# First mixer of a two-layer trunk: single-block loads behind modulation units, all units on VectorE, and norms whose roots are taken on 128x2

## The chip, the cores and the metric

The kernel runs on one core of one Trainium2 chip. The metric is the device time of one execution in microseconds (us), median of several runs; less is better. The engines are TensorE (PE, with its weight loads as PEld), VectorE (DVE), ScalarE (ACT), GpSimd (POOL) and SyncE (SP), which here only issues DMAs. Every engine takes its instructions in the order in which the program has them.

## The reference, cut to what matters

```python
for l in range(2):
    mod = (silu(c) @ ada_w[l] + ada_b[l])            # 6 vectors of 1024: sh1, sc1, g1, sh2, sc2, g2
    h = rmsnorm(x, norm_mix[l]) * (1 + sc1) + sh1
    if l % 2 == 0:                                   # first mixer
        proj = h @ ev_w_in                           # 1024 -> 1536: z (gated) and pool input
        ya = spatial_gating(gelu(proj[:, :512]), gelu(proj[:, 512:1024]))
        yb = multiscale_pool(proj[:, 1024:])
        y = concat(ya, yb) @ ev_w_out
    else:
        y = diff_attention(h, ...)
    x = x + g1 * y
    h = rmsnorm(x, norm_ffn[l]) * (1 + sc2) + sh2
    x = x + g2 * peer(h, ...)                        # queries h @ w_q, 16384 experts
out = rmsnorm(x, final_norm)
```

There are 256 tokens of width 1024, all in f32. `rmsnorm` divides each token by the root of its mean square over the 1024 features.

## The kernel before

**Layout.** `xt` holds x with the features on the partitions: 8 chunks `c` of 128 features by 256 tokens. Weights come from HBM as a stream of blocks of 128x1024 (512 KB). Blocks 0 to 11 are `ev_w_in`, 12 to 19 `ev_w_out`, 20 to 35 the `w_q` of the first expert stage. Blocks below 20 (`WHOLE`) are used as f32; every later one is split first into `hi` (a cast on ScalarE, L195) and `lo` (a subtraction on VectorE, L202), and each product then takes three matmuls. There are seven block buffers in this stage: a load of block k goes out when block k-7 has been used.

**Modulation units.** The first layer's `ada_w` comes in 24 units of 1 MB; the first mixer uses 0 to 19. In VectorE's form (`ada_next`, `ada_use`, L315) a unit costs two passes over 128x1024 with a running sum and two or three tiny instructions (`mod_done`). Units 0 to 7 give shift and scale for chunk c of the first norm, 8 to 11 the gates, 12 to 19 shift and scale of the second norm. Units 14 and 16 (`PE_UNITS`) are taken another way: `ada_rows` multiplies them on TensorE as rows, `ada_copy` moves the rows out, `ada_turn` turns them into columns. There are five unit buffers.

**Order of the loads.** The list `loads` sets what SyncE issues: `a5` is unit 5, `w6` the pair of blocks 12 and 13, `s0` the four small tensors. `issue` walks it as far as buffers are free in program order. SyncE has one queue: a load that waits for its buffer holds all those behind it.

**The stage around the change.** SyncE loads, `Norm` squares x on ScalarE and sums over the features with matmuls by a matrix of ones, so that `ss` is 128x256 with the same row on every partition; `rstd` takes root (L378) and reciprocal (L379) there. For each chunk c VectorE takes unit c and `hmod` (L585), ScalarE adds the shift (`hf`, L586), TensorE does the 12 products of `project`. Then come the gating (`vnorm`, `gating`), the pool sums (`pool_adds`, `pool_sums`) and `out_proj`. In `run_blocks` the first `lead` blocks go together, chunk by chunk: four of `ev_w_out` here, six of `w_q` (blocks 20 to 25) in the expert stage. The other four blocks of `out_proj` follow one by one, and for each finished output chunk `done` updates `xt` (L421) and squares it. `renorm` takes the second norm and `modulate`: per chunk `hmod` (L401) on VectorE, `hh[0]` on ScalarE (L403), `hh[1]` on VectorE (L394). `between` splits the last blocks ahead of the modulation, so that all six leading blocks are split when `modulate` begins.

Norms stand at five places: twice in each layer, and at the end of the kernel, where five of the eight output chunks are scaled on VectorE (L1253) and three on ScalarE and GpSimd (L1251).

Of the kernel before, what the change touches and what calls it, by code (L numbers as in the profile page):

```python
# [20 lines left out]
P = 128  # L21
# [20 lines left out]
NRAW = 4  # L42
PE_UNITS = (14, 16)
WHOLE = 20
# [3 lines left out]
def trunk(ctx, tc, xT, crow, vecs, consts_in, pos, lamv, bs, cnt, ws, wpool, ada, ev_in, ev_out,  # L48
# [293 lines left out]
    class Norm:  # L342
# [17 lines left out]

        def square(self, c):
            if self.last:
                self.add()
            q = self.buf(c)
            nc.scalar.activation(q, xt[:, c, :], AF.Square)
            self.last = (c, q)

        def sums(self):
            while self.sq:
                self.n += 1  # L370
                self.ss = self.ss if self.n > 1 else aux()
                mm(self.ss[:, :S], ones, self.sq.pop(0), self.n == 1, self.n == min(NCH, 1 + NCH - self.first))

        def rstd(self, work):
            self.add()
            self.sums()
            r = work.tile([P, S], F32, name="rstd", bufs=1)
            nc.scalar.activation(r, self.ss[:, :S], AF.Sqrt, bias=epst, scale=1.0 / D)  # L378
            nc.vector.reciprocal(r, r)  # L379
            return r  # L380

# [28 lines left out]

    def renorm(norm, l, m, work, before=None, between=None):
        r = norm.rstd(work)
        if between:
            between()
        modulate(r, l, m, work, before)

# [15 lines left out]
    def mixer0(work):  # L432
# [6 lines left out]
        cnt_t = work.tile([P, 4, 16], F32, name="cnt")  # L439
        adaq, consumed, rows = {}, set(), {}  # L440

        def small():
# [4 lines left out]

        loads = ("a0 w0 a1 w1 a8 a2 w2 a3 a9 a4 w3 a5 w4 a10 a6 w5 a7 a11 s0 w6 w7 a12 a13 w8 w9 a14 a15 a16 "
                 "w10 a17 w11 a18 a19 w12").split()
        slots = [int(v[1:]) for v in loads if v[0] == "a"]  # L450

        def issue():

            while loads:
                kind, un = loads[0][0], int(loads[0][1:])
                if kind == "s":
                    small()
                elif kind == "a":
                    n = slots.index(un)
                    if n >= 5 and slots[n - 5] not in consumed:  # L460
                        return
                    r = (work if n % 5 < 3 else adag).tile([P, 2, D], F32, name=f"adaw{n % 5}")
                    dma(r, ada[0, un].rearrange("p (a b) -> p a b", a=2))
                    adaq[un] = r
                else:
                    fetch(2 * un + 1)
                    if head["unit"] < 2 * un + 2:
                        return
                loads.pop(0)
            head.update(issue=None, ahead=3)  # L470
# [6 lines left out]
        def ada_next(un):  # L477
# [5 lines left out]
            issue()  # L483

        def ada_rows(*uns):

            ps = aux()
            for k, un in enumerate(uns):
                w = loaded(un).rearrange("p a b -> p (a b)")
                for c in range(NCH):  # L490
                    mm(ps[0:1, k * S:(k + 1) * S], ccol[:, c:c + 1], w[:, c * S:(c + 1) * S], c == 0, c == NCH - 1)
            issue()
            rows[uns] = ps

        def ada_copy(name, *uns):
            ps = rows[uns]
            rows[uns] = []
            for k in range(len(uns)):
                row = work.tile([P, S], F32, name=name, bufs=3)[0:1, :]
                nc.scalar.copy(row, ps[0:1, k * S:(k + 1) * S])  # L500
                rows[uns] += [row[:, :P], row[:, P:]]

        def ada_turn(*uns):

            row = rows.pop(uns)
            ps = aux()
            for j in range(2 * len(uns)):
                mm(ps[:, j:j + 1], row[j], ones[0:1, 0:1], True, True)
            for k, un in enumerate(uns):
                mod_done(0, un, un + 1, ps[:, 2 * k:2 * k + 2])  # L510

# [25 lines left out]
        nc.scalar.dma_start(c_dram, csil[0:1, :])  # L537
        ccol = work.tile([P, NCH], F32, name="ccol")
        nc.scalar.activation(ccol, vec[:, V_C:V_C + NCH], AF.Silu)

# [11 lines left out]
        for c in range(NCH):  # L552
            norm.square(c)
            norm.sums()
        ada_next(0)
        r = norm.rstd(work)

# [23 lines left out]
        for c in range(NCH):  # L581
            if c:
                ada_next(c)
            h = work.tile([P, S], F32, name="hmod", bufs=3)
            nc.vector.scalar_tensor_tensor(h, xt[:, c, :], scl[:, 0, 0, c:c + 1], r, op0=OP.mult, op1=OP.mult)  # L585
# [9 lines left out]
        def vnorm():  # L595
            st = work.tile([P, 2, 6], F32, name="st")
            mv = work.tile([P, 2, 2], F32, name="mv")
            for t in range(2):
                nc.vector.bn_stats(st[:, t, :], zv[:, t, :])
                nc.vector.bn_aggr(mv[:, t, :], st[:, t, :])  # L600
            nc.scalar.activation(mv[:, :, 1], mv[:, :, 1], AF.Sqrt, bias=epst, scale=1.0)
            nc.vector.reciprocal(mv[:, :, 1], mv[:, :, 1])
# [50 lines left out]
        norm = norm_of(work)  # L653
        head.update(pool=0, cap=WHOLE + 2)
        ada_next(12)

        hooks = {3: [lambda: pool_mix(0), lambda: pool_mix(1)], 4: [lambda: pool_mix(2)], 5: [lambda: pool_mix(3)]}

        def after(j):
            issue()  # L660
            if j == 1:
                ada_rows(14)
                ada_copy("hmod", 14)
                ada_next(13)
            if j == 3:
                warm()
                ada_next(15)
            if j == 4:
                ada_turn(14)
                head.update(cap=WHOLE + 4)  # L670
            if j == 5:
                warm()
                ada_next(17)

        def before(c, low):
            if c == 1:
                ada_copy("sq", 16)
                ada_turn(16)
            if c in (4, 6):
# [4 lines left out]

        def between():
            ada_rows(16)
            splits(WHOLE + 6)
            lows()

        renorm(norm, 0, 1, work, before, between)  # L690
        adag_close()

# [549 lines left out]
    with ExitStack() as es:  # L1242
# [3 lines left out]
        gains = [vec[:, V_FIN + c:V_FIN + c + 1] for c in range(NCH)]  # L1246
        for c in (1, 3, 5):
            nc.scalar.activation(o[:, c, :], xt[:, c, :], AF.Copy, scale=gains[c])
# [22 lines left out]
def _layout(i):  # L1271
# [25 lines left out]
    a["ada"] = ada.transpose(0, 1, 3, 2, 4).reshape(2, 24, P, 2 * D)  # L1297
    for un in PE_UNITS:
        a["ada"][0, un] = ada[0, un].reshape(2, P, NCH, P).transpose(3, 2, 0, 1).reshape(P, 2 * D)
    ev = f("ev_w_in")[0]  # L1300
# [39 lines left out]
```

## Time and profile before

| | |
|---|---|
| runs shown | 1868.3, 1864.81, 1868.48 us; median 1868.3 us |
| profiled execution | 1868.04 us, its span 1866.3 us |
| mean granted TensorE clock | 0.988 |
| busy share | PE 97%, PEld 88%, DVE 76%, ACT 49%, POOL 9% |
| chain that ended last | PE 92%, DVE 4%, ACT 2% |
| DMA | 375.01 MB, mean 201 GB/s |

The span runs from the first to the last instruction; 1.74 us of the profiled time lie around it. A busy PE is not a PE at its peak. The chain that ended last is followed back from the last instruction through whatever released each step, so it shows what set the end.

### The profile page before, as it was taken

Reading aid. Unit: us, or ns where it says so; the run is one execution under the profiler, and the core shown is the slowest. Engines: PE = TensorE matmul, PEld = TensorE weight load, DVE = VectorE, ACT = ScalarE, POOL = GpSimd, SP = SyncE. Lnnn points to the kernel's source line nnn. Section 1 sums busy time; section 2 is a strip of 40 time slices with the busy share of each in tenths; the row PEclk is TensorE's granted clock in tenths of the full one; section 3 lists DMA queues with packets and bytes.
Section 4 is the critical chain, followed back from the end, with each engine's and each line's share of the span. In section 5 each row is a group of like instructions: output and inputs, shape, how many; then the busy total and the mean of one; then the engine's idle time right before and its main releaser. Section 6 shows DMA issues by size and latency. Waiting matters only on the chain.

```text
span 1866.3 us, 32498 instructions
## 1 busy us (share of the span) xinstructions
PE 1817.4 (97%) x12536; PEld 1643.2 (88%) x12536; DVE 1423.1 (76%) x2969; ACT 919.5 (49%) x1427; POOL 159.9 (9%) x132
## 2 busy tenths in 40 slices
PE   8889999999999999999899899999999999999997
PEld 5669999999998888888788899999999988888885
DVE  6478897888897888887677678978888966666665
ACT  2135555454445454454476445555444455544444
POOL 0005600000000100100000057000000000000000
PEclk9989999999999999999999899999999999999999
DMA  9654555545558898888533355554555555555553
GB/s 388 270 214 153 191 186 176 170 169 170 167 168 286 290 317 295 286 285 267 173 126 112 128 178 189 186 186 166 168 170 166 171 196 192 193 196 195 192 194 113
DMA packets 99614, 375.01 MB, mean 201 GB/s; under 512 B 11330, under 2 KB 11458, under 8 KB 96004
## 3 DMA queue, kind: packets, MB, share of 16 engines
q1 hardware_dynamic: 89714, 335.88, 53.0%
q0 software_dynamic: 8304, 30.15, 4.7%
q10 hardware_dynamic: 1442, 6.92, 1.0%
q8 instruction: 98, 1.61, 0.3%
q14 instruction: 56, 0.46, 0.1%
HBM read 369.76 MB, written 3.15 MB: 200 GB/s over the span
## 4 chain that ended last, share of the span: by engine, by line
PE 92%; DVE 4%; ACT 2%; issue 1%; DMA 1%; SPq 0%; DVEq 0%; ACTq 0%
PE acc L64 46%; PE mm L64 44%; PE aux L64 2%; DVE lo L202 1%; DMA raw<-in_wq_dram 1%; ACT hi L195 0%; DVE rstd L379 0%; DVE adaw L315 0%; DVE xt L421 0%; DVE ob L1060 0%; DVE pd L613 0%; DVE on L801 0%; DVE ga L1078 0%; DVE oe L1058 0%; DVE xt L1204 0%
## 5 line engine op out<-in xcount | busy, mean ns | idle before, releaser
L64 PE MATMUL mm<-hh,hi 128*128 128x256 f32 x4640 | 818.0, 280 | 0.0
L202 DVE TENSOR_TENSOR lo<-raw,hi 128x1024 fp32r<-128x1024 f32 x526 | 640.6, 1222 | 192.4 <-ACT hi L195 189.8
L64 PEld LDWEIGHTS mm<-hh,hi 128*128 128x128 f32 x4640 | 702.3, 188 | 0.0
L195 ACT CAST hi<-raw 128x1024 fp32r<-128x1024 f32 x576 | 602.6, 1049 | 146.3 <-PE mm L64 83.2
L64 PE MATMUL mm<-hh,lo 128*128 128x256 f32 x2320 | 643.1, 277 | 0.4 <-DVE lo L202 0.4
L64 PEld LDWEIGHTS mm<-hh,lo 128*128 128x128 f32 x2320 | 435.6, 188 | 0.6 <-DVE lo L202 0.6
L64 PE MATMUL acc<-hi,ch 128*128 128x512 f32 x1024 | 277.3, 390 | 0.2 <-DVE ga L1216 0.2
L64 PE MATMUL acc<-hi,cl 128*128 128x512 f32 x1024 | 277.1, 390 | 0.0
L64 PE MATMUL acc<-lo,ch 128*128 128x512 f32 x1024 | 276.9, 390 | 0.0
L64 PEld LDWEIGHTS acc<-hi,ch 128*128 128x128 f32 x1024 | 192.1, 188 | 41.6 <-DVE ga L1216 0.7
L64 PEld LDWEIGHTS acc<-hi,cl 128*128 128x128 f32 x1024 | 192.1, 188 | 41.6 <-DVE cl L1125 0.6
L64 PEld LDWEIGHTS acc<-lo,ch 128*128 128x128 f32 x1024 | 192.2, 188 | 41.1
L1124 ACT CAST ch<-ga 128x256 fp32r<-128x256 f32 x192 | 78.1, 407 | 251.7 <-PE acc L64 251.7
L200 POOL TENSOR_TENSOR lo<-raw,hi 128x1024 fp32r<-128x1024 f32 x50 | 119.6, 2411 | 278.5 <-ACT hi L195 278.5
L1125 DVE TENSOR_TENSOR cl<-ga,ch 128x256 fp32r<-128x256 f32 x192 | 81.4, 424 | 75.3 <-ACT ch L1124 75.3
L1089 ACT ACTIVATE ga<-mm 128x512 f32<-128x512 f32 (+20 forms) x92 | 37.4, 407 | 166.6 <-PE mm L64 166.6
L1060 DVE TENSOR_TENSOR ob<-oe,xt 128x512 f16<-128x512 f16 x256 | 97.4, 421 | 4.4
L64 PE MATMUL acc<-ob,oa 128*128 128x128 f16 x1024 | 80.3, 220 | 0.4
L1092 DVE TENSOR_TENSOR ga<-mm,ga 128x48 f32<-128x48 f32 (+31 forms) x86 | 37.6, 438 | 52.0 <-ACT mm L1091 51.6
L1124 ACT CAST ch<-gb 128x256 fp32r<-128x256 f32 x64 | 25.8, 407 | 78.0 <-PE acc L64 78.0
L64 PEld LDWEIGHTS <-oa 128*128 128x128 f16 x1024 | 57.9, 98 | 5.7 <-issue 0.9
L1251 POOL TENSOR_TENSOR o<-o,rstd 128x256 f32<-128x256 f32 x3 | 2.7, 919 | 698.3 <-DVE rstd L379 698.3
(229 smaller groups left out, 1541.3 us busy)
## 6 DMA issues: line engine op xcount, KB each, us to landing
raw<-in_u_emb_dram SPq DMA_DIRECT2D x256, 512.0 KB, 3.7
raw<-in_v_emb_dram SPq DMA_DIRECT2D x256, 512.0 KB, 4.2
adaw<-in_ada_dram SPq DMA_DIRECT2D x20, 1024.0 KB, 11.3
raw<-in_wq_dram SPq DMA_DIRECT2D x32, 512.0 KB, 5.2
xt<-in_ada_dram POOLq DMA_DIRECT2D x28, 512.0 KB, 7.6
adaw<-in_ada_dram POOLq DMA_DIRECT2D x28, 512.0 KB, 5.4
raw<-in_od_in_dram SPq DMA_DIRECT2D x24, 512.0 KB, 3.5
raw<-in_ev_in_dram SPq DMA_DIRECT2D x12, 512.0 KB, 10.4
```

Source lines behind the costliest of these rows:

```text
L64: nc.tensor.matmul(out_, l, r, start=start, stop=stop, skip_group_check=True)
L195: nc.scalar.copy(hif, r)
L200: nc.gpsimd.tensor_tensor(lof[:, :m], r[:, :m], hif[:, :m].bitcast(F32), op=OP.subtract)
L202: nc.vector.tensor_tensor(lof[:, m:], r[:, m:], hif[:, m:].bitcast(F32), op=OP.subtract)
L1060: nc.vector.tensor_mul(by_two(ob[:, q]), by_two(oe), one(2 + q))
L1089: nc.scalar.activation(v[:, :, t:] if t else v, pair[:, :, t:] if t else pair, AF.Gelu)
L1092: nc.vector.tensor_mul(v[:, :, :t], pair[:, :, :t], v[:, :, :t])
L1124: nc.scalar.copy(ch, src)
L1125: nc.vector.tensor_tensor(cl, src, ch.bitcast(F32), op=OP.subtract)
L1251: nc.gpsimd.tensor_tensor(o[:, c, :], o[:, c, :], r, op=OP.mult)
```

## The change

The change has five parts. The loads from `a12` on stand in another order, and the pairs w8 and w9 become single blocks (`b16` to `b19`) with units ahead of them. Units 14 and 16 are taken on VectorE like the others; `ada_rows`, `ada_copy` and `ada_turn` go. Unit 12 moves into `vnorm`, units 13 to 16 stand right behind `pool_sums`, and the splits of blocks 20 to 23 are spread over `out_proj` (`after`); `between` is gone, and blocks 24 and 25 are split where the expert stage takes its blocks (`take`, `warm`). The first eight squares are taken on VectorE, unit 0 stands behind the first norm instead of ahead of it. And every norm sums with 128 tokens on the partitions: `ss` is 128x2, root and reciprocal are taken on that, and a diagonal matrix times ones spreads the result over the partitions into PSUM. At the end all eight output chunks are scaled on VectorE.

```diff
-        loads = ("a0 w0 a1 w1 a8 a2 w2 a3 a9 a4 w3 a5 w4 a10 a6 w5 a7 a11 s0 w6 w7 a12 a13 w8 w9 a14 a15 a16 "
-                 "w10 a17 w11 a18 a19 w12").split()
+        loads = ("a0 w0 a1 w1 a8 a2 w2 a3 a9 a4 w3 a5 w4 a10 a6 w5 a7 a11 s0 a12 w6 a13 w7 a14 a15 b16 a16 b17 b18 "
+                 "a17 a18 a19 b19 w10 w11 w12").split()
...
-        def square(self, c):
+        def square(self, c, vector=False):
...
-            nc.scalar.activation(q, xt[:, c, :], AF.Square)
+            if vector:
+                nc.vector.tensor_mul(q, xt[:, c, :], xt[:, c, :])
+            else:
+                nc.scalar.activation(q, xt[:, c, :], AF.Square)
...
-                mm(self.ss[:, :S], ones, self.sq.pop(0), self.n == 1, self.n == min(NCH, 1 + NCH - self.first))
+                q = self.sq.pop(0)
+                for t in range(2):
+                    mm(self.ss[:, t:t + 1], q[:, t * P:(t + 1) * P], ones[:, 0:1], self.n == 1 and t == 0,
+                       self.n == min(NCH, 1 + NCH - self.first))
...
-            r = work.tile([P, S], F32, name="rstd", bufs=1)
-            nc.scalar.activation(r, self.ss[:, :S], AF.Sqrt, bias=epst, scale=1.0 / D)
+            r = work.tile([P, 2], F32, name="rstd", bufs=1)
+            nc.scalar.activation(r, self.ss[:, :2], AF.Sqrt, bias=epst, scale=1.0 / D)
             nc.vector.reciprocal(r, r)
-            return r
+            dg = work.tile([P, 2, P], F32, name="rdiag", bufs=1)
+            nc.vector.tensor_tensor(dg, ident[:, None, :].to_broadcast([P, 2, P]),
+                                    r[:, :, None].to_broadcast([P, 2, P]), op=OP.mult)
+            ps = aux()
+            mm(ps[:, :S], ones, dg.rearrange("p a b -> p (a b)"), True, True)
+            return ps[:, :S]
...
-        nc.scalar.activation(ccol, vec[:, V_C:V_C + NCH], AF.Silu)
+        preload(AF.Sqrt)
...
         for c in range(NCH):
-            norm.square(c)
+            norm.square(c, vector=True)
             norm.sums()
+        r0 = norm.rstd(work)
         ada_next(0)
-        r = norm.rstd(work)
+        r = work.tile([P, S], F32, name="rstd0")
...
+            ada_next(12)
             nc.scalar.activation(mv[:, :, 1], mv[:, :, 1], AF.Sqrt, bias=epst, scale=1.0)
...
-        head.update(pool=0, cap=WHOLE + 2)
-        ada_next(12)
+        head.update(pool=0)
+        for un in range(13, 17):
+            ada_next(un)
...
         def after(j):
             issue()
-            if j == 1:
-                ada_rows(14)
-                ada_copy("hmod", 14)
-                ada_next(13)
+            if j > 3:
+                lows()
+            splits(WHOLE + (0, 0, 0, 1, 2, 4, 4, 4)[j])
             if j == 3:
-                warm()
-                ada_next(15)
-            if j == 4:
-                ada_turn(14)
-                head.update(cap=WHOLE + 4)
-            if j == 5:
-                warm()
                 ada_next(17)
...
-        def between():
-            ada_rows(16)
-            splits(WHOLE + 6)
-            lows()
-
-        renorm(norm, 0, 1, work, before, between)
+        renorm(norm, 0, 1, work, before)
...
-            if c in (1, 3, 5):
-                nc.gpsimd.tensor_tensor(o[:, c, :], o[:, c, :], r, op=OP.mult)
-            else:
-                nc.vector.scalar_tensor_tensor(o[:, c, :], xt[:, c, :], gains[c], r, op0=OP.mult, op1=OP.mult)
+            nc.vector.scalar_tensor_tensor(o[:, c, :], xt[:, c, :], gains[c], r, op0=OP.mult, op1=OP.mult)
```

SyncE's loads from the first of `ev_w_out` on, before (numbers tell unit buffers apart; the eight `in_ev_out` rows are blocks 12 to 19, the first `in_wq` ones blocks 20 and up):

```order
L170 DMA raw<-in_ev_out_dram 128x1024 x4
L463 DMA adaw_348<-in_ada_dram 128x2048
L463 DMA adaw_353<-in_ada_dram 128x2048
L170 DMA raw<-in_ev_out_dram 128x1024 x4
L463 DMA adaw_515<-in_ada_dram 128x2048
L463 DMA adaw_517<-in_ada_dram 128x2048
L463 DMA adaw_519<-in_ada_dram 128x2048
L170 DMA raw<-in_wq_dram 128x1024 x2
```

The same place in the changed kernel:

```order
L471 DMA adaw_340<-in_ada_dram 128x2048
L169 DMA raw<-in_ev_out_dram 128x1024 x2
L471 DMA adaw_362<-in_ada_dram 128x2048
L169 DMA raw<-in_ev_out_dram 128x1024 x2
L471 DMA adaw_372<-in_ada_dram 128x2048
L471 DMA adaw_391<-in_ada_dram 128x2048
L169 DMA raw<-in_ev_out_dram 128x1024
L471 DMA adaw_411<-in_ada_dram 128x2048
L169 DMA raw<-in_ev_out_dram 128x1024 x2
L471 DMA adaw_437<-in_ada_dram 128x2048
L471 DMA adaw_494<-in_ada_dram 128x2048
L471 DMA adaw_500<-in_ada_dram 128x2048
L169 DMA raw<-in_ev_out_dram 128x1024
L169 DMA raw<-in_wq_dram 128x1024 x16
```

Block 19 now stands behind all units instead of ahead of six of them; blocks 14 and 15 stand behind units 12 and 13.

VectorE at the end of the second norm's modulation, with the expert stage's next splits behind it, before:

```order
L394 SCALAR_TENSOR_TENSOR hh_96<-hmod,mod_92,hh_95 128x256
L401 SCALAR_TENSOR_TENSOR hmod<-xt,scl,rstd 128x256
L394 SCALAR_TENSOR_TENSOR hh_96<-hmod,mod_92,hh_95 128x256 x2
L202 TENSOR_TENSOR lo<-raw,hi 128x1024 x3
L939 MAX ga<-ga 128x8 x2
```

The same place in the changed kernel:

```order
L405 SCALAR_TENSOR_TENSOR hh_96<-hmod,mod_92,hh_95 128x256
L412 SCALAR_TENSOR_TENSOR hmod<-xt,scl,aux 128x256
L405 SCALAR_TENSOR_TENSOR hh_96<-hmod,mod_92,hh_95 128x256 x2
L201 TENSOR_TENSOR lo<-raw,hi 128x1024 x5
L910 MAX ga<-ga 128x8 x2
```

Behind the modulation five splits stand instead of three: those of blocks 24 and 25, which stood between the norm's reciprocal and the first `hmod`, are the first two of them now. ScalarE's casts for them moved in the same way.

TensorE's first rows, before:

```order
L64 MATMUL mm<-vn,ones 128x512 x2
L64 MATMUL aux<-sq,ones 128x256 x8
L64 MATMUL acc_107<-raw,hf 128x512
L64 MATMUL acc_108<-raw,hf 128x512
L64 MATMUL acc_109<-hf,raw 128x256 x2
```

And in the changed kernel:

```order
L63 MATMUL mm<-vn,ones 128x512 x2
L63 MATMUL aux<-ones,sq 128x1 x16
L63 MATMUL aux<-rdiag,ones 128x256
L63 MATMUL acc_107<-raw,hf 128x512
L63 MATMUL acc_108<-raw,hf 128x512
```

Eight wide products became sixteen of one column, each with the squares as weights, and one wide product more stands ahead of the projection.

## Rows read from the trace of the kernel before

**Rows 1.** The page's chain that ended last, shares of the span by engine:

```profile
PE 92%; DVE 4%; ACT 2%; issue 1%; DMA 1%; SPq 0%; DVEq 0%; ACTq 0%
```

**Rows 2.** That chain from 60 to 180 us: start, length, what:

```profile
84.54 11.57 DMA raw<-in_wq_dram
...
118.53 2.29 DVE lo L202 x2
...
124.31 16.76 PE acc L64 x127
141.09 1.06 ACT hi L195
```

**Rows 3.** Timeline of SP: start, length, queue, line, issues merged:

```profile
55.30 27.16 SPq L170 DMA_DIRECT2D raw<-in_ev_out_dram  x4
```

**Rows 4.** Windows: length, busy PE, PEld, DVE, ACT, POOL, PE clock, DMA, GB/s:

```profile
0.00:63.50 63.50, 54.07 (x181) 37.41 (x181) 40.23 (x89) 17.81 (x32) 3.98 (x15) 0.95 0.99 394
...
67.00:83.00 16.00, 15.41 (x70) 12.78 (x69) 9.00 (x25) 1.90 (x4) 0.00 (x0) 1.00 0.03 12
...
16.00:17.00 1.00, 0.00 (x0) 0.00 (x0) 0.96 (x2) 0.00 (x0) 0.00 (x0) 0.55 1.08 455
```

**Rows 5.** Timeline of PE (an f32 product is two instructions):

```profile
7.91 6.07 PE L64 MATMUL aux<-sq,ones 128*128 128x256 f32 x16 [1.76 <-ACT sq L365]
17.68 3.78 PE L64 MATMUL acc<-raw,hf 128*128 128x512 f32 x4 [3.71 <-ACT hf L586]
...
100.04 0.60 PE L64 MATMUL aux<-ones,hmod 1*128 1x1 f32 x4 [3.16 <-ACT hmod L500]
...
105.81 7.07 PE L64 MATMUL mm<-yy,raw 128*128 128x256 f32 x32
...
122.06 1.01 PE L64 MATMUL aux<-ones,sq 1*128 1x1 f32 x4 [2.20 <-ACT sq L500]
...
1057.80 1.19 PE L64 MATMUL aux<-sqt,ones 128*128 128x256 f32 x2 [2.62 <-DVE sqt L356]
```

**Rows 6.** Timeline of PEld, weight loads:

```profile
18.70 0.34 PEld L64 LDWEIGHTS acc<-raw,hf 128*128 128x128 f32 x1 [0.52 <-issue]
...
1847.63 1.03 PEld L1200 LDWEIGHTS mm<-ident,ga 128*128 128x128 f32 x8
```

**Rows 7.** Timeline of DVE:

```profile
14.82 1.75 DVE L379 RECIPROCAL rstd<-rstd 128x256 f32<-128x256 f32 x1 [2.60 <-ACT rstd L378]
...
62.54 0.17 DVE L602 RECIPROCAL mv<-mv 128x2 f32<-128x2 f32 x1 [2.52 <-ACT mv L601]
...
73.79 1.22 DVE L315 SCALAR_TENSOR_TENSOR adaw<-adaw,csil 128x1024 f32<-128x1024 f32 x1
...
99.14 1.22 DVE L315 SCALAR_TENSOR_TENSOR adaw<-adaw,csil 128x1024 f32<-128x1024 f32 x1
...
101.82 0.48 DVE L421 SCALAR_TENSOR_TENSOR xt<-acc,mod,xt 128x256 f32<-128x256 f32 x1
...
102.54 0.48 DVE L421 SCALAR_TENSOR_TENSOR xt<-acc,mod,xt 128x256 f32<-128x256 f32 x1
...
125.76 1.21 DVE L315 SCALAR_TENSOR_TENSOR adaw<-adaw,csil 128x1024 f32<-128x1024 f32 x1
...
134.55 0.48 DVE L394 SCALAR_TENSOR_TENSOR hh<-hmod,mod,hh 128x256 fp32r<-128x256 f32 x1 [0.18 <-ACT hh L403]
...
1063.03 0.88 DVE L401 SCALAR_TENSOR_TENSOR hmod<-xt,scl,rstd 128x256 f32<-128x256 f32 x2
...
1065.69 0.48 DVE L394 SCALAR_TENSOR_TENSOR hh<-hmod,mod,hh 128x256 fp32r<-128x256 f32 x1
```

**Rows 8.** Timeline of ACT:

```profile
62.23 0.28 ACT L601 ACTIVATE mv<-mv,epst 128x2 f32<-128x2 f32 x1
...
135.19 0.34 ACTq L907 DMA_DIRECT2D ga<-in_sk_dram  x1
```

**Rows 9.** Line L1253, the last scalings: duration ns min/median/max, first and last start:

```profile
L1253 DVE SCALAR_TENSOR_TENSOR o<-xt,vec,rstd x5: 473/941/943, 1857.8 to 1860.8; 128x256 f32<-128x256 f32 x5
```

More of the change, by code (lines that the diff above doesn't have):

```diff
@@ L42 @@
 NRAW = 4
-PE_UNITS = (14, 16)
 WHOLE = 20
@@ L409, in modulate, with renorm @@
         low()
-    def renorm(norm, l, m, work, before=None, between=None):
-        r = norm.rstd(work)
-        if between:
-            between()
-        modulate(r, l, m, work, before)
+    def renorm(norm, l, m, work, before=None):
+        modulate(norm.rstd(work), l, m, work, before)
     def out_proj(l, y, order, norm, hooks={}, after=None):
@@ L439, in mixer0 @@
         cnt_t = work.tile([P, 4, 16], F32, name="cnt")
-        adaq, consumed, rows = {}, set(), {}
+        adaq, consumed = {}, set()
         def small():
@@ L465, in issue @@
                 else:
-                    fetch(2 * un + 1)
-                    if head["unit"] < 2 * un + 2:
+                    last = un if kind == "b" else 2 * un + 1
+                    fetch(last)
+                    if head["unit"] <= last:
                         return
@@ L483, in ada_next @@
             issue()
[L485 to L510, printed above, removed]
         late_lo = []
@@ L537, in mixer0 @@
         nc.scalar.dma_start(c_dram, csil[0:1, :])
-        ccol = work.tile([P, NCH], F32, name="ccol")
-        nc.scalar.activation(ccol, vec[:, V_C:V_C + NCH], AF.Silu)
+        preload(AF.Sqrt)
         pad = work.tile([P, 4, 16 + S], F32, name="pad")
@@ L552, in mixer0 @@
         for c in range(NCH):
-            norm.square(c)
+            norm.square(c, vector=True)
             norm.sums()
+        r0 = norm.rstd(work)
         ada_next(0)
-        r = norm.rstd(work)
+        r = work.tile([P, S], F32, name="rstd0")
         proj = {k: (acc[k] if k < 4 else mm_tile().rearrange("p a b -> p (a b)")) for k in range(6)}
@@ L584, in mixer0 @@
             h = work.tile([P, S], F32, name="hmod", bufs=3)
-            nc.vector.scalar_tensor_tensor(h, xt[:, c, :], scl[:, 0, 0, c:c + 1], r, op0=OP.mult, op1=OP.mult)
+            nc.vector.scalar_tensor_tensor(h, xt[:, c, :], scl[:, 0, 0, c:c + 1], r if c else r0,
+                                           op0=OP.mult, op1=OP.mult)
+            if not c:
+                nc.vector.tensor_copy(r, r0)
             nc.scalar.activation(hf[:, c, :], h, AF.Identity, bias=mod[0][:, c:c + 1])
@@ L660, in after @@
             issue()
-            if j == 1:
-                ada_rows(14)
-                ada_copy("hmod", 14)
-                ada_next(13)
+            if j > 3:
+                lows()
+            splits(WHOLE + (0, 0, 0, 1, 2, 4, 4, 4)[j])
             if j == 3:
-                warm()
-                ada_next(15)
-            if j == 4:
-                ada_turn(14)
-                head.update(cap=WHOLE + 4)
-            if j == 5:
-                warm()
                 ada_next(17)
         def before(c, low):
-            if c == 1:
-                ada_copy("sq", 16)
-                ada_turn(16)
             if c in (4, 6):
@@ L1246, in trunk @@
         gains = [vec[:, V_FIN + c:V_FIN + c + 1] for c in range(NCH)]
-        for c in (1, 3, 5):
-            nc.scalar.activation(o[:, c, :], xt[:, c, :], AF.Copy, scale=gains[c])
         for c in range(NCH):
-            if c in (1, 3, 5):
-                nc.gpsimd.tensor_tensor(o[:, c, :], o[:, c, :], r, op=OP.mult)
-            else:
-                nc.vector.scalar_tensor_tensor(o[:, c, :], xt[:, c, :], gains[c], r, op0=OP.mult, op1=OP.mult)
+            nc.vector.scalar_tensor_tensor(o[:, c, :], xt[:, c, :], gains[c], r, op0=OP.mult, op1=OP.mult)
             if c % 2:
@@ L1297, in _layout @@
     a["ada"] = ada.transpose(0, 1, 3, 2, 4).reshape(2, 24, P, 2 * D)
-    for un in PE_UNITS:
-        a["ada"][0, un] = ada[0, un].reshape(2, P, NCH, P).transpose(3, 2, 0, 1).reshape(P, 2 * D)
     ev = f("ev_w_in")[0]
```

## The prediction, made blind

> **What bounds the kernel now.** I read the chain that ended last first: TensorE holds 92% of it [rows 1], so a saving elsewhere counts only where TensorE waits. Then I followed the chain in order of time. After the first mixer it is TensorE almost throughout; inside the mixer it leaves TensorE for a transfer of 11.57 us from 84.54 on, and for splits on VectorE between the second norm and the expert stage. Its first long piece of TensorE there runs from 124.31 to 141.07: the six leading blocks 20 to 25. ScalarE's next cast follows at 141.09, and that end is the mark against which I work [rows 2].
>
> Third, SyncE's timeline gives the reason for the transfer: four loads of `ev_w_out` take it from 55.30 to 82.46, since block 19 waits for a buffer until `out_proj` has finished its four leading blocks at about 83 [rows 3]. Units 14 and later stand behind it. The windows agree: 394 GB/s on average up to 63.5 us, 12 GB/s from 67 to 83, while TensorE is busy 15.41 of those 16 us [rows 4]. VectorE idles there too. So the kernel loses its time after 83, and the change fills the hole ahead of it.
>
> **The change part by part.** All times from here are on the scale of the profiled execution.
>
> *The start.* The sums took 16 instructions in 6.07 us [rows 5]. Now there are 32 with one moving column and a weight load of 128 columns each. No row shows one with 128 partitions of weights. The nearest are the four single-column instructions that turned the rows of units 14 and 16: 0.60/4 = 0.15 us at the full 2.4 GHz, 1.01/4 = 0.25 us at 1.2 GHz [rows 5]. Thus 4.8 to 8.1 us. The old sums, at 0.43 each when slow and 0.22 when fast (half of 1.19/2, and 7.07/32, [rows 5]; 1.19 includes the filling), would be 6.9 or 3.5 us, so their 6.07 means about three quarters slow; the same mix gives 7.3 us. Squares on VectorE can begin a little earlier than on ScalarE; I put the sums' start at 7.5 instead of 7.91 and their end at 14.8 (bounds 12.3 and 15.6).
>
> The Trainium skill ("TensorE: Matmul & The Clock Gate", section "LDWEIGHTS (loading the stationary operand)") says that a weight load lasts as its columns do, whatever the number of rows, and puts it at columns over 1.2, about 0.107 us here. On the rows the traces agree: eight full 128x128 loads took 1.03 us, 0.13 each [rows 6], near the 0.15 with one row. With 0.107 us, an estimate from that page, the sums would end near 11 us and the forecast would come out 3.8 us lower. The rows decide, since the slow ones are plainly longer.
>
> Then come root 0.28 [rows 8] and reciprocal 0.17 [rows 7] on 128x2 and the diagonal, which like an update of 0.48 passes over 128x256: with small hops 0.98. Unit 0 now stands behind these on VectorE, 2.68 us (99.14 to 101.82, [rows 7]), and its cover by the squares is gone; the spreading product lies under it. From the end of the old reciprocal, 16.57, to the projection at 17.68 is 1.11 us [rows 5, 7]. So the projection starts at 14.8 + 0.98 + 2.68 + 1.11 = 19.6, **1.9 us later** (bounds -0.6 and +2.7). The granted clock averaged 0.55 from 16 to 17 us, after TensorE had idled since 13.98: it had fallen to 1.2 GHz before the projection began [rows 4, 5]. If the new product kept it at 2.4, the first chunk would not be slow; its first four instructions alone took 3.78 us, half of that at the full clock. I take the low level again, and allow 2.7 us of gain in the lower bound.
>
> *The gating.* Unit 12 fills VectorE's wait of 2.52 us ahead of the reciprocal [rows 7]; at 2.68 plus a hop it delays that by 0.2. **In sum 2.1 us late** up to the end of the pool sums. The data are there: up to blocks 14 and 15 the new order moves 14 units of 1.05 MB, 16 blocks of 0.52, x with 1.05 and 0.9 of small tensors, 25.0 MB, at 394 GB/s 63.5 us. TensorE was busy without much of a gap from 67 on [rows 4], and `out_proj` now begins 2.1 later than it did then.
>
> *VectorE through `out_proj`.* Its start, 73.79 [rows 7], becomes 75.9. Units 13 to 16: 4 x 2.68 = 10.7, to 86.6. Updates 0 to 3: two at 0.4, two with their addition at 0.72 (101.82 to 102.54, [rows 7]), 2.2; unit 17; to 91.5. Updates 4 to 6, 2.2, and four splits at 2.29/2 = 1.15 [rows 2], 4.6: 98.3. TensorE needs as long: leading blocks done at 83 + 2.1, then four blocks at 7.07/2 = 3.53 [rows 5], 99.2. The last update ends at 99.7. Loads keep up: block 19 has 10 us after its buffer comes free, the `w_q` blocks follow it. Unit 14 as rows, its wait for data, and the old order of splits are all gone from here.
>
> *The second norm.* Square 0.4, four last narrow products 0.6, root, reciprocal and diagonal 0.98, spreading product 0.6 to 1.2, say 1.0: `hmod` starts at 102.7, against 120.8 before, where the splits of 24 and 25 ended [rows 2]. But now these two come behind it, and too late. The modulation keeps VectorE for 3.06 us up to unit 18 (1063.03 to 1065.69 and one pitch of 0.40) and from there, with units 18 and 19, 134.55 + 0.48 - 125.76 = 9.27: to 115.0 [rows 7]. ScalarE issued the load of `ga` at 135.19, just behind VectorE's last `hh` [rows 7, 8]; the casts of 24 and 25 stand behind it. So 0.5 for it, two casts at 1.06 [rows 2], then a split of 1.15: block 25 is ready at 118.7. TensorE does chunk 0 of blocks 20 to 23 at 104 and then stands for 13 us, as block 24 is next in its order.
>
> It starts cold then, as it did at 124.31. That piece took 16.76 us for eight chunks with waits inside; seven chunks, cold again, I put at 16.4. The leading blocks end at 135.1 against 141.07: **6.0 us earlier**. Behind that the stream of products is the same, and TensorE's share of the chain says that the shift stays.
>
> *The other norms.* The reciprocal's 1.75 becomes 0.17 [rows 7] and the root some 0.2 shorter; the diagonal with 0.48 and the spreading product with 0.6 to 1.2 are added, sums get 0.4 to 0.8 longer. That is -0.3 at full clock, +0.2 at half: nothing for the two of layer 1 together (-0.1). At the end the scalings on VectorE took 0.94 us beside GpSimd and 0.47 alone [rows 9]; eight at some 0.43 replace five that began between 1857.8 and 1860.8: about -0.4 with the norm. **In sum -0.5.**
>
> 1868.04 - 6.0 - 0.5 = **1861.5 us**. The median of the runs shown is 0.3 above the profiled time, so the same number stands against it.
>
> **The rivals.**
> 1. *The narrow sums run slow, and it gets slower.* A 128x128 load took 0.34 us in the cold projection [rows 6]. If it does not lie beside its own instruction of 0.25, each costs 0.59 and the sums 18.9 us, so the projection starts 11.6 us later than forecast: 1873. It decides from 0.43 us each, where the whole gain is gone. Against it: loads and single columns took 0.25 together at the slow clock.
> 2. *Little of it arrives.* The sums at 0.33 to 0.4, or the leading blocks at the low clock for 3 us more: 1864.5 to 1868. For it: two cold starts, neither shown here.
> 3. *The late splits cost nothing.* TensorE would run from 104 on and end the leading blocks near 121, 14 us earlier still: 1847. Against it: the order of the rows, with block 24 ahead of chunk 1 of all others.
> 4. *The clock stays up through the first norm*, or the sums run at 0.15: 1857 to 1859.
>
> **How the numbers follow.** A measurement of this kernel can tell 0.2%, 3.7 us, from no change. The forecast, 1859 to 1864.5, has 0.56; rival 4 has 0.11, rival 3 has 0.03; rival 2 and everything else within 3.7 us has 0.22; rival 1 and other losses 0.08. So faster 0.70, same 0.22, slower 0.08. The range from 1857 to 1867 leaves out rivals 1 and 3 and the end of rival 2; the likeliest case's own range is 1859 to 1864.5.
>
> **What would show it.** Right: no hole in the transfers between 67 and 83, VectorE without a gap from 76 to 98, the last update near 100, a wait of 10 us or more of TensorE near 105 that ends with a cast or split of block 24 or 25, the leading blocks done near 135, and 0.25 us for a narrow product at the first norm. Wrong: sums at the start beyond 10 us, no wait at 105, or a later stage that takes the 6 us back.

## The result, and the profile after

The changed kernel takes 1858.6 us, median of 8 runs (1851.86 to 1860.66), against 1867.65 us for the kernel before (8 runs, 1864.81 to 1868.79): a ratio of 0.9946, 95% interval 0.9931 to 0.9961, or 9.1 us less. The profiled execution took 1858.97 us, its span 1857.3.

The page's chain that ended last, of the changed kernel (line numbers from here on are those of the changed kernel or of the experiment):

```profile
PE 89%; DVE 3%; ACT 1%; issue 1%; DVEq 0%; ACTq 0%
```

The shares add up to 94% only, because the profile follows this chain back no further than 116.8 us; they can't be set against those of [rows 1]. The chain from 60 to 180 us:

```profile
116.87 15.20 PE acc L63 x111
...
132.09 1.06 ACT hi L194
```

The mark of the prediction, ScalarE's cast behind the leading blocks, stands at 132.09 instead of 141.09 [rows 2]. So the whole 9.0 us are there at the end of the first mixer. Where this text says that the leading blocks end, it means this mark, as the prediction does. Their last products run some 1.6 us past it in both kernels: the first product behind them starts at 133.70, before at 142.71, so the difference is the same. Its windows, with the columns of [rows 4]; the last one belongs to the first expert stage and is needed further down:

```profile
67.00:83.00 16.00, 15.56 (x72) 13.16 (x71) 15.31 (x38) 1.90 (x4) 0.00 (x0) 1.00 0.98 391
101.00:114.00 13.00, 3.24 (x12) 2.71 (x12) 11.34 (x28) 4.59 (x9) 0.00 (x0) 0.51 0.49 187
...
184.50:234.50 50.00, 50.00 (x427) 50.00 (x426) 40.42 (x143) 25.27 (x30) 24.12 (x11) 1.00 0.57 187
```

The hole is gone: 391 GB/s where there were 12, and VectorE is busy for 15.31 of those 16 us instead of 9.00. Behind it a new hole has come, on TensorE: 3.24 us of work between 101 and 114, at a granted clock of 0.51, the lower level of 1.2 GHz. VectorE's timeline shows what goes on there:

```profile
97.15 0.48 DVE L429 SCALAR_TENSOR_TENSOR xt<-mm,mod,xt 128x256 f32<-128x256 f32 x1 [0.29 <-PE mm L63]
...
100.55 0.87 DVE L412 SCALAR_TENSOR_TENSOR hmod<-xt,scl,aux 128x256 f32<-128x256 f32 x2 [0.79 <-PE aux L63]
...
112.36 0.49 DVE L405 SCALAR_TENSOR_TENSOR hh<-hmod,mod,hh 128x256 fp32r<-128x256 f32 x1 [0.18 <-ACT hh L414]
114.45 2.36 DVE L201 TENSOR_TENSOR lo<-raw,hi 128x1024 fp32r<-128x1024 f32 x2 [1.61 <-ACT hi L194]
...
1850.74 3.22 DVE L1219 SCALAR_TENSOR_TENSOR o<-xt,vec,aux 128x256 f32<-128x256 f32 x8 [1.38 <-PE aux L63]
```

The last update ends at 97.6, the modulation runs from 100.55 to 112.85, and only then come the splits of blocks 24 and 25, the two `lo` at 114.45. TensorE's timeline:

```profile
6.66 6.99 PE L63 MATMUL aux<-ones,sq 128*128 128x1 f32 x32 [0.26 <-DVE sq L365]
...
18.48 3.78 PE L63 MATMUL acc<-raw,hf 128*128 128x512 f32 x4 [2.60 <-ACT hf L571]
...
25.90 1.88 PE L63 MATMUL acc<-raw,hf 128*128 128x512 f32 x4
...
101.62 1.10 PE L63 MATMUL acc<-hh,hi 128*128 128x256 f32 x2 [1.11 <-ACT hh L414]
...
114.47 0.79 PE L63 MATMUL acc<-hh,hi 128*128 128x256 f32 x2 [9.61 <-ACT hi L194]
...
913.38 4.15 PE L63 MATMUL aux<-ones,ga 128*128 128x1 f32 x20 [0.45 <-DVE ga L355]
...
921.07 1.10 PE L63 MATMUL acc<-hh,hi 128*128 128x256 f32 x2 [1.12 <-ACT hh L414]
...
1056.08 1.10 PE L63 MATMUL acc<-hh,hi 128*128 128x256 f32 x2 [1.12 <-ACT hh L414]
...
1840.76 1.03 PE L1171 MATMUL mm<-ident,ga 128*128 128x128 f32 x8
```

The rows of the kernel before that answer to the later ones, TensorE's timeline too:

```profile
25.54 1.88 PE L64 MATMUL acc<-raw,hf 128*128 128x512 f32 x4
...
922.85 2.43 PE L64 MATMUL aux<-ga,ones 128*128 128x256 f32 x10 [0.45 <-DVE ga L356]
...
928.74 1.10 PE L64 MATMUL acc<-hh,hi 128*128 128x256 f32 x2 [3.46 <-ACT hh L403]
...
1064.12 1.10 PE L64 MATMUL acc<-hh,hi 128*128 128x256 f32 x2 [3.41 <-ACT hh L403]
...
1847.86 1.03 PE L1200 MATMUL mm<-ident,ga 128*128 128x128 f32 x8
```

Set side by side these rows say where the lead was won and lost:

| place | before | after | difference |
|---|---|---|---|
| second chunk of the projection | 25.54 | 25.90 | +0.4 |
| cast behind the leading blocks | 141.09 | 132.09 | -9.0 |
| first sum of layer 1's first norm | 922.85 | 913.38 | -9.5 |
| first product behind that norm | 928.74 | 921.07 | -7.7 |
| first product behind layer 1's second norm | 1064.12 | 1056.08 | -8.0 |
| last stage turned | 1847.86 | 1840.76 | -7.1 |
| end of the span | 1866.3 | 1857.3 | -9.0 |

Layer 1's first norm gave 1.8 us back, and from the last stage's turning on 1.9 were won. That the two nearly cancel is chance.

### The profile page after: what moved, and what is told of

It reads as the page before. It is cut to its first block, busy times and chain, and to the rows that moved or that the text cites. A ratio compares the mean times of both kernels' runs of the same rounds, so it can differ in the third digit from the quotient of the medians.

```text
span 1857.3 us, 32546 instructions
## 1 busy us (share of the span) xinstructions
PE 1815.0 (98%) x12554; PEld 1648.9 (89%) x12554; DVE 1425.5 (77%) x2994; ACT 914.4 (49%) x1414; POOL 157.6 (8%) x129
## 4 chain that ended last, share of the span: by engine, by line
PE 89%; DVE 3%; ACT 1%; issue 1%; DVEq 0%; ACTq 0%
PE acc L63 44%; PE mm L63 43%; PE aux L63 1%; DVE lo L201 1%; ACT hi L194 0%; DVE ob L1031 0%; DVE on L772 0%; DVE ga L1049 0%; DVE o L1219 0%; DVE oe L1029 0%; DVE xt L1175 0%; DVE oa L1028 0%; DVE ga L1063 0%; ACT ga L367 0%; ACT mm L1062 0%
## 5 line engine op out<-in xcount | busy, mean ns | idle before, releaser
L63 PE MATMUL acc<-hh,hi 128*128 128x256 f32 x224 | 48.1, 317 | 13.0 <-ACT hi L194 9.6
## 6 DMA issues: line engine op xcount, KB each, us to landing
adaw<-in_ada_dram SPq DMA_DIRECT2D x20, 1024.0 KB, 12.6
```

Of the source, the lines that this page charges most:

```text
L63: nc.tensor.matmul(out_, l, r, start=start, stop=stop, skip_group_check=True)
```

## The experiments

Each was timed beside the kernel before. A median stands beside a ratio to those runs; the medians of before lay between 1866.8 and 1868.1.

| kernel | median us | ratio to before | 95% interval |
|---|---|---|---|
| the change | 1858.6 | 0.9946 | 0.9931 to 0.9961 |
| before + order of the loads | 1863.57 | 0.9990 | 0.9977 to 1.0002 |
| before + units on VectorE | 1870.42 | 1.0023 | 1.0013 to 1.0033 |
| change, splits bunched | 1863.65 | 0.9978 | 0.9967 to 0.9990 |
| change, late splits ahead of the modulation | 1848.39 | 0.9916 | 0.9900 to 0.9932 |
| change, late splits behind chunk 0 | 1845.0 | 0.9871 | 0.9855 to 0.9888 |
| the same, unit 0 ahead of the first norm | 1839.62 | 0.9863 | 0.9845 to 0.9882 |
| change, wide norms | 1856.68 | 0.9955 | 0.9939 to 0.9971 |
| the change again | 1857.91 | 0.9953 | 0.9937 to 0.9969 |
| change, unit 0 ahead of the first norm | 1855.56 | 0.9947 | 0.9928 to 0.9966 |
| change, first squares on ScalarE | 1858.85 | 0.9959 | 0.9945 to 0.9974 |

**Where the gain comes from.** Is it the order of the loads? First the kernel before with that part alone:

```diff
-        loads = ("a0 w0 a1 w1 a8 a2 w2 a3 a9 a4 w3 a5 w4 a10 a6 w5 a7 a11 s0 w6 w7 a12 a13 w8 w9 a14 a15 a16 "
-                 "w10 a17 w11 a18 a19 w12").split()
+        loads = ("a0 w0 a1 w1 a8 a2 w2 a3 a9 a4 w3 a5 w4 a10 a6 w5 a7 a11 s0 a12 w6 a13 w7 a14 a15 b16 a16 b17 b18 "
+                 "a17 a18 a19 b19 w10 w11 w12").split()
...
```

> The kernel before with nothing but the new order of the loads (single blocks behind units); units 14 and 16 stay on TensorE, splits stay ahead of the modulation, norms stay wide. If the gain of the change comes from the hole in the transfers: no transfer of 11.6 us on the chain from 84.5, 300 GB/s or more between 67 and 83, out_proj done near 100 instead of 113, the leading blocks done 8 to 14 us earlier than 141.1, and 1854 to 1860 us. Rival (the order pays only with units 14 and 16 on VectorE, since their rows on TensorE wait for VectorE's hmod and for the blocks): TensorE waits 5 us or more between 83 and 100, and the kernel gains under 5 us, 1863 to 1868.

It gains little, if anything, since the interval reaches 1.0002, and neither theory had the reason. The windows show 270 GB/s between 67 and 83, so most of the hole is filled. The leading blocks still end at 136.98, only 4.1 earlier than before. Its timeline of SyncE:

```profile
74.89 10.67 SPq L463 DMA_DIRECT2D adaw<-in_ada_dram  x3
```

The same three loads in SyncE's timeline of the change:

```profile
64.75 14.79 SPq L471 DMA_DIRECT2D adaw<-in_ada_dram  x3
```

VectorE and TensorE, with the loads alone again:

```profile
96.34 1.23 DVE L202 TENSOR_TENSOR lo<-raw,hi 128x1024 fp32r<-128x1024 f32 x1 [9.91 <-ACT hi L195]
...
110.20 0.48 DVE L421 SCALAR_TENSOR_TENSOR xt<-mm,mod,xt 128x256 f32<-128x256 f32 x1
```

```profile
110.34 1.22 PE L64 MATMUL aux<-sqt,ones 128*128 128x256 f32 x2 [10.39 <-DVE sqt L356]
```

Three unit loads take SyncE from 74.89 to 85.56: it waits for unit buffers, 10.6 us of it for VectorE's `mod`, the end of a unit. The blocks of `w_q` behind them go out from 86.09 on. In the change these loads take even longer, 14.79 us, but from 64.75 on, and `w_q` goes out from 82.90, 3.2 us earlier than here. The larger difference is on VectorE. It has its next split in its order, block 20's, already at 86.4 and stands for 9.91 us with ready units and updates behind it; in the change it comes to that split at 90.77, behind the units, and does not wait. The wait has moved from TensorE's block 16 to VectorE's split.

The other half is units 14 and 16 on VectorE in the old order of the loads:

```diff
...
             if j == 1:
-                ada_rows(14)
-                ada_copy("hmod", 14)
                 ada_next(13)
+                ada_next(14)
...
         def between():
-            ada_rows(16)
+            ada_next(16)
             splits(WHOLE + 6)
             lows()
```

> The kernel before with the other half of the change: units 14 and 16 are taken on VectorE (unit 14 behind 13 in out_proj, unit 16 behind the second norm's reciprocal), the order of the loads stays. If the two halves pay only together: the hole in the transfers between 67 and 83 stays, unit 14's data still come at about 88, VectorE carries 2.7 us more ahead of the modulation, and the kernel takes 1866 to 1871 us, no gain. Rival (VectorE instead of TensorE for these units is itself the gain): 1863 us or less, the leading blocks done by 137.

1870.42: slower by 3.5 us, as the first theory had it. VectorE's timeline before, from the wait on, and then VectorE's and TensorE's with the units alone:

```profile
95.98 2.46 DVE L202 TENSOR_TENSOR lo<-raw,hi 128x1024 fp32r<-128x1024 f32 x2 [19.42 <-ACT hi L195]
...
114.58 0.48 DVE L421 SCALAR_TENSOR_TENSOR xt<-mm,mod,xt 128x256 f32<-128x256 f32 x1
```

```profile
96.47 2.46 DVE L202 TENSOR_TENSOR lo<-raw,hi 128x1024 fp32r<-128x1024 f32 x2 [19.32 <-ACT hi L195]
...
117.49 0.48 DVE L421 SCALAR_TENSOR_TENSOR xt<-mm,mod,xt 128x256 f32<-128x256 f32 x1
```

```profile
117.63 1.22 PE L64 MATMUL aux<-sqt,ones 128*128 128x256 f32 x2 [20.26 <-DVE sqt L356]
```

VectorE stands for 19.32 us ahead of the same split, as it does before (19.42), but now unit 14 follows there too, and the last update ends at 118.0 instead of 115.1. TensorE, without that unit's rows, is through with its products earlier and waits 20.26 us for VectorE. Unit 16 stands between reciprocal and modulation in this kernel, not behind the pool sums as in the change, so this is not quite the change's other half. The halves need each other: the loads can go out early only if VectorE consumes units early, and VectorE has units to consume only if they were loaded. The third part, the spreading of the splits, is taken back here:

```diff
-            if j > 3:
-                lows()
-            splits(WHOLE + (0, 0, 0, 1, 2, 4, 4, 4)[j])
+            splits(WHOLE + (0, 0, 0, 2, 2, 4, 4, 4)[j])
+            lows()
```

> The changed kernel with the splits of blocks 20 to 23 bunched as before: 20 and 21 both behind the update of chunk 3 and ahead of unit 17, 22 and 23 behind the update of chunk 5. If it matters that no split stands on VectorE ahead of its block's arrival: block 20 lands at 89.7, so VectorE, which now goes without a gap from 74 to 97, waits some 3.5 us from 87.3 on; the last update ends near 101 instead of 97.6, the leading blocks near 136 instead of 132.1, and the kernel takes 1861 to 1864 us. Rival (VectorE has slack behind it, or TensorE's last blocks end last there): the last update within 1 us of 97.6, and 1858 to 1860.

1863.65, 5 us of the gain lost. VectorE's timeline:

```profile
92.17 2.50 DVE L201 TENSOR_TENSOR lo<-raw,hi 128x1024 fp32r<-128x1024 f32 x2 [3.23 <-ACT hi L194]
...
102.96 0.48 DVE L429 SCALAR_TENSOR_TENSOR xt<-mm,mod,xt 128x256 f32<-128x256 f32 x1
```

It waits 3.23 us for block 20, and the last update ends at 103.4, which is 5.8 later than in the change; 0.9 of that is a later arrival of x in this execution. The leading blocks end at 138.49. VectorE has no slack there. This kernel also closes the square of the two halves: the last update ends at 115.1 before, at 110.7 with the loads alone, at 118.0 with the units alone, and at 103.4 with both, though that kernel has the change's start and norms as well. The new loads with spread splits but without the units were not run.

**What the late splits cost.** Now the 9.61 us. First the two splits go back to where they were:

```diff
...
-        modulate(norm.rstd(work), l, m, work, before)
+        r = norm.rstd(work)
+        if between:
+            between()
+        modulate(r, l, m, work, before)
...
+        def between():
+            splits(WHOLE + 6)
+            lows()
...
```

> The changed kernel, with the splits of blocks 24 and 25 put back between the second norm's reciprocal and the modulation. If these two late splits are what holds TensorE from 104.9 to 114.5: no wait of 9.6 us there. Block 25's load is issued only at 97.1 and lands near 102 to 103, so its split ends near 105 and the first hmod starts there instead of at 100.6; the leading blocks then end near 122 to 125 instead of 132.1, and the kernel takes 1850 to 1853 us, 6 to 9 below the changed kernel. Rival (the record's rival 2 in another form: the wait for block 25's load takes the place of the wait for its split): hmod starts after 108 and the time stays within 2 us of the changed kernel's 1858.6.

1848.39, 10 us less than the change. Its chain:

```profile
96.88 0.33 SPq L169
...
97.26 4.86 DMA raw<-in_wq_dram
...
102.14 1.05 ACT hi L194
...
103.21 1.23 DVE lo L201
104.44 0.40 DVE hmod L412
...
105.43 17.63 PE acc L63 x128
123.08 1.06 ACT hi L194
```

TensorE's eight chunks run without a stop, 17.63 us. But block 25's load, issued at 96.88, now holds the modulation back by 3.9 us. TensorE needs that block only after its chunk 0 of blocks 20 to 23. So the splits belong behind chunk 0 of the modulation:

```diff
         def before(c, low):
+            if c == 1:
+                low()
+                splits(WHOLE + 6)
+                lows()
             if c in (4, 6):
```

This was run with unit 0 ahead of the first norm as well, and then alone.

> The changed kernel with unit 0 ahead of the first norm, and with the splits of blocks 24 and 25 behind the modulation's chunk 0: behind the first hmod and hh, ahead of the second hmod. If the two splits must only be ready when TensorE has done chunk 0 of blocks 20 to 23 (3 us at the low clock), and block 25 lands at 102: the modulation starts near 99.1, TensorE has no wait over 1.5 us behind it, the leading blocks end near 117 to 120 (132.1 in the change, 123.1 with the splits ahead of the modulation), and the kernel takes 1843.5 to 1847 us. Rival (the splits in between hold chunk 1 back, so that TensorE waits 3 us or more there): the leading blocks end near 122 or later, and the time is that of the splits ahead of the modulation, 1847 to 1849.

> The changed kernel with one edit: the splits of blocks 24 and 25 behind the modulation's chunk 0; unit 0 stays behind the first norm. If this edit alone carries the gain: the leading blocks end near 119 to 121, 11 to 13 us ahead of the change, and the kernel takes 1840 to 1846 us, at most 2 above the run that also had unit 0 ahead. That run gained another 3.1 us between 121 and 540, where TensorE took 443 products in 50 us instead of 427 at the same granted clock: if the earlier start of the expert stage causes it, 440 or more again; if it was a matter of that one execution, 427 to 430 and 1843 to 1847. Rival to the whole: the leading blocks end at 123 or later, and 1848 or more.

Alone 1845.0, with the other edit 1839.62; the intervals of the two ratios overlap. The chain of the run with one edit:

```profile
101.28 18.15 PE acc L63 x128
119.45 1.06 ACT hi L194
```

The chunks start at 101.28, as early as in the change, and run through: the leading blocks end 12.6 us ahead of it. That is the price of the late splits, told by one edit. Both edits together have the lowest median of all, 19 us under the change, with a ratio of 0.9863 to before.

In that run the lead over the change grows by another 3.1 us, from 13.1 at the mark to 16.2 at the first sum of layer 1's first norm. A window of it that answers to the change's from 184.5 on:

```profile
171.30:221.30 50.00, 50.00 (x443) 50.00 (x443) 41.42 (x147) 26.14 (x30) 24.17 (x11) 1.00 0.59 193
```

There are 443 products in 50 us, where the change has 427, at a granted clock of 1.00 in both. The run with one edit starts the stage within half a microsecond of this one and has 427 again, so the earlier start does not explain it.

**The norms.** The change with wide norms at all five places:

```diff
-                q = self.sq.pop(0)
-                for t in range(2):
-                    mm(self.ss[:, t:t + 1], q[:, t * P:(t + 1) * P], ones[:, 0:1], self.n == 1 and t == 0,
-                       self.n == min(NCH, 1 + NCH - self.first))
+                mm(self.ss[:, :S], ones, self.sq.pop(0), self.n == 1, self.n == min(NCH, 1 + NCH - self.first))
```

The root and the reciprocal are then taken on 128x256 again, without diagonal and spreading product.

> The changed kernel with the wide norms of before at all five places (sums over 128x256, root and reciprocal on 128x256); squares at the start and the order of unit 0 as in the change. If the narrow norms brought nothing or cost a little, as the trace after says (layer 1's first norm 7.7 us from its first sum to the next product against 5.9 before): 1856 to 1858.5 us, up to 2.5 below the changed kernel, with 5.9 us at that norm again. Rival (the small roots and reciprocals are where the last microseconds of the gain come from): 1860 us or more, the projection at the start 1 to 2 us later.

1856.68 with an interval that holds the change's ratio: the norms as a whole move less than can be told. TensorE's timeline:

```profile
7.07 6.78 PE L63 MATMUL aux<-sq,ones 128*128 128x256 f32 x16 [1.02 <-DVE sq L365]
19.88 3.78 PE L63 MATMUL acc<-raw,hf 128*128 128x512 f32 x4 [6.04 <-ACT hf L559]
...
915.06 2.43 PE L63 MATMUL aux<-ga,ones 128*128 128x256 f32 x10 [0.45 <-DVE ga L355]
920.95 1.10 PE L63 MATMUL acc<-hh,hi 128*128 128x256 f32 x2 [3.47 <-ACT hh L405]
```

At the start the narrow form saves 1.0 us from the first sum to the projection (6.66 to 18.48 against 7.07 to 19.88). At layer 1's first norm the wide one takes 5.89 us again, where the change took 7.69. Is that the form or the clock? The change itself ran once more:

> The changed kernel itself once more, for a second trace. If the 1.8 us that layer 1's first norm lost in the first trace come from the clock alone, which fell to half inside the twenty narrow sums there: this norm takes either 5.9 us (full clock) or 7.7 us (half) from its first sum to the next product, nothing in between by more than 0.3, and the span differs from the first trace's by about this and what the second norm shows. Rival (the narrow norm is longer for another reason): 7.7 us again at a full clock. Time 1855 to 1860 either way.

```profile
915.15 3.94 PE L63 MATMUL aux<-ones,ga 128*128 128x1 f32 x20 [0.45 <-DVE ga L355]
...
922.63 1.10 PE L63 MATMUL acc<-hh,hi 128*128 128x256 f32 x2 [1.11 <-ACT hh L414]
```

7.48 us, again slow. TensorE's timeline with the splits ahead of the modulation, and a window of the change inside its sums:

```profile
904.00 2.39 PE L63 MATMUL aux<-ones,ga 128*128 128x1 f32 x20 [0.45 <-DVE ga L355]
```

```profile
914.00:915.00 1.00, 1.00 (x6) 1.00 (x7) 0.51 (x2) 0.96 (x3) 0.00 (x0) 0.50 0.00 0
```

The twenty sums took 2.39 us, and the norm 5.9, in the traces with the splits ahead of the modulation, with unit 0 ahead, with unit 0 ahead and the splits behind chunk 0, and with the splits bunched. In these the granted clock is 1.00 through nearly all of the sums. They took 4.15 and 3.94 in the change, 3.36 with the splits behind chunk 0, 2.80 with the squares on ScalarE. In these last four the granted clock falls from 1.00 to 0.50 inside the sums, in the change within their first microsecond. So it is the clock, and values in between come from where in the sums it falls; my "nothing in between" was wrong. At the full clock the narrow norm takes as long here as the wide one. In the four traces with wide sums at this place (before, loads alone, units alone, wide norms) they took 2.42 or 2.43 each time.

**The start.** Unit 0 ahead of the first norm again:

```diff
-        r0 = norm.rstd(work)
         ada_next(0)
+        r0 = norm.rstd(work)
```

> The changed kernel with unit 0 ahead of the first norm's root again. If unit 0 behind the norm costs what stands on VectorE between the diagonal and hmod (2.7 us less the spreading product of 1.2): the projection starts near 17.2 instead of 18.5, and if the stages behind it follow, the kernel takes 1857 to 1858 us, about 1 below the changed kernel. Rival (the start is covered, by the clock that rises later or by the data): the projection starts earlier, its second chunk does not, and the time stays at 1858.6 within 0.4.

```profile
17.12 3.78 PE L63 MATMUL acc<-raw,hf 128*128 128x512 f32 x4 [1.11 <-ACT hf L571]
...
24.38 1.88 PE L63 MATMUL acc<-raw,hf 128*128 128x512 f32 x4
```

The projection starts 1.4 us earlier and its second chunk 1.5. The leading blocks end 1.6 earlier, so nothing covers it. The time, 1855.56 over runs from 1850.09 to 1859.05, does not tell it from the change. Last, the first squares on ScalarE, by `norm.square(c)` without the argument:

> The changed kernel with the first eight squares back on ScalarE. If the narrow sums are paced by TensorE (0.22 each, 7.0 us in all) and only their start depends on the squares: first sum at 7.7 to 8.2 instead of 6.7, the projection about 1.2 later, and 1859 to 1861 us, which the scatter of the runs will hardly tell from 1858.6. Rival (ScalarE's squares are slower than the sums and pace them): the sums take 8 us or more, the projection 2 us or more later.

ScalarE's and TensorE's timelines:

```profile
7.25 1.28 ACT L287 ACT_TABLE_LOAD   x1 [0.55 <-ACT csil L518]
```

```profile
9.11 6.99 PE L63 MATMUL aux<-ones,sq 128*128 128x1 f32 x32 [3.04 <-ACT sq L367]
```

The sums take 6.99 us with either engine, so TensorE paces them. They start 2.5 us later, not 1.2: the change also loads the table for the root ahead, and on ScalarE the squares stand behind that load of 1.28. The time, 1858.85, is that of the change.

## Why the prediction held, and where its sizes were off

**The hole and VectorE.** As forecast, the transfers have no hole, VectorE works without a gap from 74 to 97, and the last update ends at 97.6 (forecast 99.7). What the prediction told too simply is why: it named block 19 on SyncE's queue. The runs show that the order of the loads and the units on VectorE pay in full only together, and that the spreading of the splits adds 5 us. With the loads alone the queue stands for unit buffers, with the units alone for block 19, and a split ahead of its block's arrival stops VectorE either way.

**The late splits.** Forecast: TensorE does chunk 0 of blocks 20 to 23 and stands for 13 us until block 24 is cast. Measured: it does that and stands for 9.61, released by the cast of block 24. The 13 was counted from the start of chunk 0, at 104; from there to block 24 it is 12.85 us (101.62 to 114.47), of which the chunk itself takes 3.2. The modulation lasted 12.3 us as forecast. Rival 3, in which the late splits cost nothing, is out: one edit showed that they cost 12.6 us. The forecast's own way of counting thus named a loss of that size, which the change still has.

**The terms that were mis-sized.** The time, 1858.6, lies in the stated range from 1857 to 1867, but 0.4 below the forecast's own, 1859 to 1864.5. Against the forecast of -6.0 the leading blocks ended 9.0 earlier. Two terms make nearly all of the 3.0:

- *The start*, put at +1.9 and with the gating at +2.1. The sums ran nearly as counted (6.99 us for 7.3, 0.22 each), but began at 6.66 for 7.5, since VectorE's squares follow x directly. The projection started at 18.48, not 19.6. The first chunk, taken as slow as before, was 0.4 shorter. The second chunk came 0.36 late, so some 1.7 of the 2.1 did not arise. The 0.43 us for a slow wide sum, from which the 7.3 were mixed, does not follow from half of 1.19/2, which is 0.30; the value itself fits, since with wide norms sixteen took 6.78 us at the start, 0.42 each. The 0.107 us of the Trainium skill ("TensorE: Matmul & The Clock Gate", section "LDWEIGHTS (loading the stationary operand)"), by which the sums would have ended near 11, is close to what the sums of layer 1 took at a granted clock of 1.00, 2.39/20 = 0.12 us. At the start they took 0.22, and the rows were the better guide.
- *The seven chunks*, put at 16.4 from the split of block 25 to the mark, took 15.20.

**The other norms and the tail.** Forecast -0.1 for layer 1 and -0.4 at the end. Layer 1's first norm cost 1.8, by the clock. The prediction had put a norm at half clock at +0.2, but its own terms (-1.58, -0.2, +0.48, +1.2, +0.8) add up to +0.7, and a fall of the clock inside the sums was not among them. The end gained: from the last stage's first turning row to the end of the span there are 18.4 us before and 16.5 after. With wide norms but all scalings on VectorE it is 16.5 too, with the loads alone, and so the old scalings, 18.4. So the scalings gain 1.9, the norm nothing, but not by the step that I counted: eight alone on VectorE take 3.22, about as long as the five beside GpSimd [rows 9], and the last one ends only 0.2 earlier after that first turning row. The rest lies behind the last transfer's issue. The three traces with scalings on GpSimd have 18.4 or 18.5 us there, the nine without 16.5 to 16.7; what is waited for at the end no view shows.

**The rivals.** Rival 1 needed 0.43 us for each narrow sum; they took 0.22 at the slowest. Rival 2 did not come: the sums took 0.22, not 0.33 or more, and the seven chunks 1.2 us less than counted. Rival 4's time is the one that was measured, but not by its mechanism: the sums were slow and the first chunk began slow. That the number fell into its range is chance.

**What stays open.** The spans of the two stages between (-9.0 to -9.5 in the first expert stage, -8.0 to -7.1 in the second) differ by half a microsecond to one without a wait that the profile names. How much of the gain falls to the units and how much to the place of the splits is known only at the last update.

## What to carry to other kernels

When a transfer ends a wait, ask which engine's consumption lets that transfer go out; here a new order of the queue without a new order of its consumer mostly moved the wait. On an engine that runs in order, work on data that have not arrived belongs behind all work whose data have. And the latest harmless place of a preparing step is read from its consumer: here the splits had to be ready after chunk 0 of four blocks, and the earlier place cost 3.6 us at the mark and the later one 12.6.

## What was not expected of the hardware

- The same stretch of the first expert stage ran at two rates. In three of the twelve traces (loads alone, splits bunched, splits behind chunk 0 with unit 0 ahead) TensorE took 443 or 444 products in 50 us over some 90 us, in the others 427 to 430, with the granted clock at 1.00 in both. It is worth about 3 us. Whether it changes from run to run of one kernel, and so makes part of the scatter, is not shown: the change's two traces both have 427. Its cause was not found.
- An f32 product of one column with 128x128 weights, two instructions, took 0.24 us at a granted clock of 1.00 (twenty instructions in 2.39) and 0.42 where it averaged 0.54 (4.15).
- In layer 1's first norm the clock fell within the narrow sums in four of eight traces, and within the wide ones in none of four. So few traces don't show that the form is the reason, and that was not tried.
- The record of the granted clock seems to miss a low stretch at the start: the change's windows show 1.00 from 2 to 24, though its first four projection instructions take 3.78 us as they do before, where the record shows 0.50.
